# A gather kernel in which 96 rows are copied from HBM to HBM one by one, with their indices in registers

One core of one Trainium2 chip. The metric is the device time of one execution in microseconds (us), lower is better.

## The reference

```python
def setup_inputs():
    batch, seq, dim = 32, 512, 1024
    return {"x": randn(batch, seq, dim) as float32,
            "indices": randint(0, seq, (batch, 128)) as int32}

def reference(x, indices):
    for b in range(batch):
        result[b] = x[b, indices[b]]        # (32, 128, 1024) float32
```

Each of the 32 batches picks 128 rows of 4 KB out of 512. The draw is fixed; a batch has 109 to 120 distinct rows.

## The kernel before

Batches 0 to 4 are gathered whole from HBM (the chip's main memory) into SBUF (on-chip memory) and stored. From batch 5 on only distinct rows are gathered: VectorE finds repeats and gives each distinct row a slot, an indirect DMA on GpSimd fetches the slots (a slot without a row has an index out of bounds and is skipped: the trace has 3024 rows of 4 KB for the 27 x 128 slots, and 4-byte packets for the other 432), TensorE spreads the slots to the 128 output places with a 0/1 matrix, ScalarE copies the result from PSUM, where TensorE leaves it, to SBUF, and SyncE (SP) stores. Distinct rows are about 114 of 128, so this saves about a tenth of the reads. (Of batch 5 only the rows from 256 up are gathered; ScalarE's queue loads the lower 256 whole beforehand.) The table `rank` says which slot the n-th distinct row takes, so that the 16 DMA engines get the same number of rows (189 each, by the count in the prediction below).

```python
    rank = const.tile([N, 8, 16], I32, name="rank")
    for e in range(8):
        fold = 0
        for bit, col in enumerate((6, 5, 3)):
            fold ^= col * (e >> bit & 1)
        steps = [[(-16 if fold >> bit & 1 else 16) << bit, 2] for bit in (2, 1, 0)]
        nc.gpsimd.iota(rank[:, e], pattern=[[1, 2]] + steps, base=2 * e + 16 * fold, channel_multiplier=0)
    # ... cut
    def store(b):
        if b not in PAIRED:
            nc.sync.dma_start(out=of[b * N:(b + 1) * N], in_=blocks[b])
        elif b % 2:
            nc.sync.dma_start(out=of[(b - 1) * N:(b + 1) * N].rearrange("(t p) d -> p t d", t=2),
                              in_=blocks[b - 1, "pair"][:])

    for b in range(HEAD):                     # HEAD = 5
        gather(blocks[b], first[...] if b == 0 else idxT[:, b:b + 1], b)
        store(b)
    # ... cut: ranks, slots, the 0/1 matrices
    def fetch(b):
        if HEAD <= b < B:
            gather(held[(b - HEAD) % RING][:], at[:, b:b + 1], b, bounds_check=S - 1, oob_is_err=False)
    # ... cut
    for b in range(HEAD, B):
        spread_rows(b)                        # matmuls, PSUM to SBUF, store(b)
        fetch(b + RING)                       # RING = 8
```

Of the kernel before, what the change touches and what calls it, by code (L numbers as in the profile page):

```python
# [6 lines left out]
F32 = mybir.dt.float32  # L7
F16 = mybir.dt.float16
I32 = mybir.dt.int32
ALU = mybir.AluOpType  # L10
# [18 lines left out]
def kernel(ctx, tc, x, indices, out):  # L29
# [14 lines left out]
    nc = tc.nc  # L44
    B, S, D = x.shape
    N = indices.shape[1]
    HEAD, RING, GROUP, AHEAD, FAR = 5, 8, 3, 4, 1024
    HALF = HEAD
    PAIRED = range(12, 20)
    GROUPS = (B - HEAD) // GROUP  # L50
    assert 2 * N <= S <= FAR and (B - HEAD) % GROUP == 0
    const = ctx.enter_context(tc.tile_pool(name="const", bufs=1))
    ring = ctx.enter_context(tc.tile_pool(name="ring", bufs=1))
    rows = ctx.enter_context(tc.tile_pool(name="rows", bufs=1))
    pick = ctx.enter_context(tc.tile_pool(name="pick", bufs=1))
    junkp = ctx.enter_context(tc.tile_pool(name="junk", bufs=4))
    PS = bass.MemoryType.PSUM
    pbc = ctx.enter_context(tc.tile_pool(name="pbc", bufs=2, space=PS))
    psm = ctx.enter_context(tc.tile_pool(name="psm", bufs=1, space=PS))
    pout = ctx.enter_context(tc.tile_pool(name="pout", bufs=4, space=PS))  # L60
    pe, dve, act = InOrder(tc), InOrder(tc), InOrder(tc)
    mm, v = nc.tensor.matmul, nc.vector


    first = const.tile([N, 1], indices.dtype, name="first")
    nc.sync.dma_start(out=first[:], in_=indices.rearrange("b n -> n b")[:, 0:1])
    vals = const.tile([B, N], indices.dtype, name="vals")
    nc.sync.dma_start(out=vals[:], in_=indices)


    diff = const.tile([N, N], I32, name="diff")
    nc.gpsimd.iota(diff[:], pattern=[[1, N]], base=0, channel_multiplier=-1)
    rank = const.tile([N, 8, 16], I32, name="rank")
    for e in range(8):
        fold = 0
        for bit, col in enumerate((6, 5, 3)):
            fold ^= col * (e >> bit & 1)
        steps = [[(-16 if fold >> bit & 1 else 16) << bit, 2] for bit in (2, 1, 0)]
        nc.gpsimd.iota(rank[:, e], pattern=[[1, 2]] + steps, base=2 * e + 16 * fold, channel_multiplier=0)
    less = const.tile([N, 1], F32, name="less")  # L80
    zero = const.tile([N, 1], F32, name="zero")
    dve(v.memset, zero[:], 0.0)
# [4 lines left out]
    above = const.tile([N, N], F16, name="above")  # L87
    dve(v.tensor_scalar, out=above[:], in0=diff[:], scalar1=0, scalar2=None, op0=ALU.is_gt)
    dve(v.tensor_copy, out=less[:], in_=diff[:, 0:1])
    every = const.tile([N, N], F16, name="every")  # L90
    dve(v.memset, every[:], 1.0)
    turn = const.tile([N, N], F16, name="turn")
    dve(v.tensor_copy, out=turn[:], in_=rank[:].rearrange("p e q -> p (e q)"))
    vf = const.tile([N, N], F16, name="vf")
    dve(v.memset, vf[:], 0.0)
    dve(v.tensor_copy, out=vf[:B],
        in_=vals[:].bitcast(I32).rearrange("p (n two) -> p n two", two=2)[:, :, 0])
# [4 lines left out]
    for k in range(2):  # L102
        load = act(nc.scalar.dma_start, out=early[k][:], in_=xf[HALF * S + k * N:HALF * S + (k + 1) * N])
        if k == 0:
# [7 lines left out]
    idxT = const.tile([N, B], I32, name="idxT")  # L112
# [3 lines left out]
    near = const.tile([N, B], F16, name="near")  # L116
    dve(v.tensor_scalar, out=near[:], in0=tr[:], scalar1=float(-FAR), scalar2=None, op0=ALU.add)

    of = out.flatten_outer_dims()

    def gather(dst, at, b, **kw):
        nc.gpsimd.indirect_dma_start(  # L122
            out=dst, out_offset=None,
            in_=xf[:], in_offset=bass.IndirectOffsetOnAxis(ap=at, axis=0),
            element_offset=b * S * D, **kw)


    blocks = {}
    for b in range(B):
        if b not in PAIRED:  # L130
            blocks[b] = rows.tile([N, D], F32, name=f"block{b}")[:]
# [4 lines left out]

    def store(b):
        if b not in PAIRED:
            nc.sync.dma_start(out=of[b * N:(b + 1) * N], in_=blocks[b])
        elif b % 2:  # L140
            nc.sync.dma_start(out=of[(b - 1) * N:(b + 1) * N].rearrange("(t p) d -> p t d", t=2),
                              in_=blocks[b - 1, "pair"][:])

    for b in range(HEAD):
        gather(blocks[b], first[:].bitcast(I32)[:, 0:1] if b == 0 else idxT[:, b:b + 1], b)
        store(b)

    def table(name, dtype):
        return const.tile([N, B], dtype, name=name)

    cnt, lead, slot = table("cnt", F32), table("lead", F16), table("slot", F16)
    nth, at = table("nth", I32), table("at", I32)
    past = const.tile([N, B + 1], F16, name="past")
    dve(v.memset, past[:, HEAD:HEAD + 1], 0.0)
    bcs, packs, spread = {}, {}, {}

    def of_group(g):
        return range(HEAD + g * GROUP, HEAD + (g + 1) * GROUP)

    def cols(t, g):  # L160
        return t[:, HEAD + g * GROUP:HEAD + (g + 1) * GROUP]

    def wide(t):
        return t.rearrange("p (g o) -> p g o", o=1).to_broadcast([N, GROUP, N])

    def step0(g):

# [3 lines left out]
        for k, b in enumerate(of_group(g)):  # L171
            junk = junkp.tile([N, N], F16, name="junk")
            dve(v.scalar_tensor_tensor, out=junk[:], in0=bc[:, k], scalar=idxF[:, b:b + 1], in1=below[:],
                op0=ALU.is_equal, op1=ALU.mult, accum_out=cnt[:, b:b + 1])
        if HALF in of_group(g):
            c = slice(HALF, HALF + 1)
            dve(v.scalar_tensor_tensor, out=cnt[:, c], in0=idxF[:, c], scalar=2.0 * N, in1=cnt[:, c],
# [4 lines left out]

    def step1(g):

        rk = psm.tile([N, GROUP], F32, name="rk")
        pe(mm, rk[:], lhsT=above[:], rhs=cols(lead, g), start=True, stop=False)
        pe(mm, rk[:], lhsT=every[:], rhs=cols(past, g), start=False, stop=True)
        dve(v.tensor_copy, out=cols(nth, g), in_=rk[:])
        dve(v.tensor_scalar, out=cols(nth, g), in0=cols(nth, g), scalar1=N - 1, scalar2=None, op0=ALU.bitwise_and)
        dve(v.scalar_tensor_tensor, out=cols(slot, g), in0=cols(cnt, g), scalar=256.0, in1=cols(nth, g),  # L190
            op0=ALU.mult, op1=ALU.add)
        packs[g] = pack = junkp.tile([N, GROUP, N], F16, name="pack")
        dve(v.tensor_tensor, out=pack[:], in0=turn[:].rearrange("p (o n) -> p o n", o=1).to_broadcast([N, GROUP, N]),
            in1=wide(cols(slot, g)), op=ALU.is_equal)

    def step2(g):

        pos = psm.tile([N, GROUP], F32, name="pos")
        for k, b in enumerate(of_group(g)):
            pe(mm, pos[:, k:k + 1], lhsT=packs[g][:, k], rhs=near[:, b:b + 1], start=True, stop=True)  # L200
        dve(v.tensor_scalar, out=cols(at, g), in0=pos[:], scalar1=float(FAR), scalar2=None, op0=ALU.add)
        s = pick.tile([N, GROUP, N], F32, name=f"s{g}")
        dve(v.tensor_tensor, out=s[:], in0=bcs[g][:, :GROUP], in1=wide(cols(at, g)), op=ALU.is_equal)
        for k, b in enumerate(of_group(g)):
            spread[b] = s[:, k]

    def fetch(b):
        if HEAD <= b < B:
            gather(held[(b - HEAD) % RING][:], at[:, b:b + 1], b, bounds_check=S - 1, oob_is_err=False)

    held = []
# [5 lines left out]
    def half_spread():  # L217

        same = pick.tile([N, 2, N], F32, name="same")
        for k in range(2):  # L220
            dve(v.tensor_scalar, out=same[:, k], in0=bcs[0][:, HALF - HEAD], scalar1=less[:], scalar2=float(k * N),
                op0=ALU.add, op1=ALU.is_equal)
        spread[HALF, "early"] = [same[:, k] for k in range(2)]

    def half_rows(h, last):
        w = slice(h * 512, (h + 1) * 512)
        if not last:
            spread[HALF, h] = pout.tile([N, 512], F32, name="ps")
        ps = spread[HALF, h]
        if last:  # L230
            pe(mm, ps[:], lhsT=spread[HALF], rhs=held[(HALF - HEAD) % RING][:, w], start=False, stop=True)
        else:
            for k in range(2):
                pe(mm, ps[:], lhsT=spread[HALF, "early"][k], rhs=early[k][:, w], start=k == 0, stop=False)
        if last:
            nc.scalar.copy(out=blocks[HALF][:, w], in_=ps[:])  # L236

    def spread_rows(b):
        for h in range(2):
            if b == HALF:  # L240
                half_rows(h, True)
                continue
            w = slice(h * 512, (h + 1) * 512)
            ps = pout.tile([N, 512], F32, name="ps")
            pe(mm, ps[:], lhsT=spread[b], rhs=held[(b - HEAD) % RING][:, w], start=True, stop=True)
            nc.scalar.copy(out=blocks[b][:, w], in_=ps[:])  # L246
        store(b)

    step0(0)
    step0(1)  # L250
    for g in range(AHEAD):
# [8 lines left out]
            half_spread()  # L260
        elif g < 3:
            half_rows(g - 1, False)
    for b in range(HEAD, B):
        spread_rows(b)
        fetch(b + RING)
        g, step = divmod(b - HEAD, GROUP)
        if g + AHEAD < GROUPS:
            (step0, step1, step2)[step](g + AHEAD)
# [30 lines left out]
```

## Time and profile before

| | before |
|---|---|
| time, median | 88.11 us (87.52 to 88.28) |
| span of the profiled run | 85.4 us |
| bytes moved, mean rate | 32.91 MB, 385 GB/s |
| 4 KB packets for one DMA engine | 501, each 159 ns |
| DMAs issued by SP | 2 loads and 28 stores |

The prediction below shows the lines for the DMA engines, stage by stage. One more view: the list of instructions that touch the output. Columns: issuing line and queue, operation, count, then the shortest, median and longest time that the issuing sequencer spends on one (ns), then start of the first and the last (us):

```profile
L139 SPq DMA_DIRECT2D out_dram<-block x24: 332/332/360, 7.2 to 78.4; - x24
L141 SPq DMA_DIRECT2D out_dram<-pair x4: 372/374/387, 40.9 to 52.3; - x4
```

### The profile page before, as it was taken

The page shows a single profiled execution, that of the slowest core. Times are in us where ns is not written, and L with a number is a line of the kernel's source. Part 1 is how long each engine was busy: PE and PEld are TensorE (multiplying, and loading weights), DVE is VectorE, ACT ScalarE, POOL GpSimd, SP SyncE. Part 2 cuts the span into 40 slices and gives each one's busy share as a digit, 9 for nine tenths or more (in the row PEclk, how much of TensorE's full clock was granted, in tenths as well). Part 3 has the DMA queues.
Part 4 walks back from the last instruction along what each step waited for, and adds up shares of the span by engine and source line. Part 5 has one row for each costly group of instructions (what it writes and reads, how often), then busy time and mean ns, then how long its engine had stood idle before and what let it go on. Part 6 is the DMA issues. An engine that isn't in the chain of part 4 may idle for free.

```text
span 85.4 us, 829 instructions
## 1 busy us (share of the span) xinstructions
PE 61.1 (72%) x189; PEld 25.5 (30%) x189; DVE 31.7 (37%) x160; ACT 40.6 (48%) x63; POOL 33.9 (40%) x45
## 2 busy tenths in 40 slices
PE   0310379460999999999999999997879988884000
PEld 0300142220434444354444444442212333320000
DVE  3698892864318547375485473000000000000000
ACT  0999920000145566656655666675553454445000
POOL 7687777837024554444555544466000000000000
PEclk9999999999569999999999999999999999999655
DMA  0999999999999999999999999999999999999990
GB/s 1 319 401 263 259 405 413 417 413 426 416 416 424 411 420 420 413 428 418 411 424 416 411 418 418 416 424 418 413 424 418 413 428 413 418 424 418 414 372 23
DMA packets 9636, 32.91 MB, mean 385 GB/s; under 512 B 1584, under 2 KB 1616, under 8 KB 9632
## 3 DMA queue, kind: packets, MB, share of 16 engines
q1 hardware_dynamic: 4736, 16.81, 48.3%
q0 software_dynamic: 4608, 15.01, 45.0%
q10 hardware_dynamic: 288, 1.05, 3.4%
q8 instruction: 1, 0.02, 0.1%
q14 instruction: 3, 0.02, 0.1%
HBM read 17.86 MB, written 16.78 MB: 406 GB/s over the span
## 4 chain that ended last, share of the span: by engine, by line
PE 39%; DMA 21%; DVE 11%; issue 8%; POOL 7%; another core or an unknown queue 2%; ACT 1%; POOLq 1%; SPq 0%; DVEq 0%
PE ps L24 36%; DMA u<-in_x_dram,at 20%; POOL u L122 7%; DVE junk L24 3%; DMA vals<-in_indices_dram 2%; DVE past L24 2%; PE bc L24 2%; DVE pack L24 1%; DVE s L24 1%; DVE nth L24 1%; PE pos L24 1%; DVE lead L24 1%; ACT block L246 1%; DVE same L24 1%
## 5 line engine op out<-in xcount | busy, mean ns | idle before, releaser
L24 PE MATMUL ps<-u,s 128*128 128x512 f32 x108 | 52.8, 624 | 3.4 <-DMA u<-in_x_dram,at 3.4
L122 POOL DMA_INDIRECT u<-in_x_dram,at x27 | 26.9, 998 | 23.8 <-PE ps L24 7.2
L246 ACT COPY block<-ps 128x512 f32<-128x512 f32 x36 | 21.1, 586 | 16.5 <-PE ps L24 15.4
L24 PEld LDWEIGHTS ps<-u,s 128*128 128x128 f32 x108 | 18.9, 193 | 24.7 <-issue 13.4
L246 ACT COPY pair<-ps 128x512 f32<-128x512 f32 x16 | 9.4, 586 | 5.8 <-PE ps L24 4.2
L24 DVE SCALAR_TENSOR_TENSOR junk<-bc,idxF,below 128x128 f16<-128x128 f32 x27 | 8.0, 347 | 7.9 <-PE bc L24 7.9
L24 ACT COPY u<-zero 128x1024 f32<-128x1024 f32 x8 | 7.7, 1040 | 0.0
L236 ACT COPY block<-ps 128x512 f32<-128x512 f32 x2 | 1.2, 586 | 13.2 <-PE ps L24 13.2
L24 PE MATMUL pos<-near,pack 128*128 128x1 f16 x27 | 2.0, 167 | 7.4 <-DVE nth L24 2.9
L24 PE MATMUL ps<-early,same 128*128 128x512 f32 x8 | 5.7, 855 | 0.0
L24 DVE TENSOR_TENSOR pack<-turn,slot 128x384 f16<-128x384 f16 x9 | 5.0, 558 | 0.3
L24 DVE TENSOR_TENSOR s<-bc,at 128x384 f32<-128x384 f32 x9 | 5.0, 557 | 0.3
L24 PEld LDWEIGHTS <-pack 128*128 128x128 f16 x27 | 1.7, 99 | 11.2 <-DVE pack L24 4.3
L24 DVE TENSOR_TENSOR past<-past,lead 128x1 f16<-128x1 f16 x27 | 4.4, 163 | 0.9
L122 POOL DMA_INDIRECT block<-in_x_dram,idxT x4 | 4.1, 1036 | 1.2 <-issue 0.9
L24 PE MATMUL bc<-vf,ident 128*128 128x128 f16 x27 | 3.5, 257 | 1.3 <-DVE same L24 1.3
L24 PEld LDWEIGHTS <-ident 128*128 128x128 f16 x27 | 2.5, 114 | 4.9 <-issue 4.9
L24 DVE TENSOR_SCALAR at<-pos 128x3 int32<-128x3 f32 x9 | 1.4, 160 | 4.2 <-PE pos L24 3.5
L24 DVE CAST nth<-rk 128x3 int32<-128x3 f32 x9 | 1.4, 159 | 4.0 <-PE rk L24 1.9
L21 PE MATMUL pos<-ident,vf 128*128 128x32 f16 x1 | 0.2, 208 | 3.2 <-DVE vf L24 3.2
L24 PE MATMUL rk<-lead,above 128*128 128x3 f16 x9 | 1.6, 172 | 1.1 <-DVE lead L24 1.1
L24 ACT ACT_TABLE_LOAD x1 | 1.3, 1283 | 2.2 <-DVE ident L24 2.2
(31 smaller groups left out, 18.4 us busy)
## 6 DMA issues: line engine op xcount, KB each, us to landing
out_dram<-block SPq DMA_DIRECT2D x24, 512.0 KB
out_dram<-pair SPq DMA_DIRECT2D x4, 1024.0 KB
early<-in_x_dram ACTq DMA_DIRECT2D x2, 512.0 KB
u<-in_x_dram,at POOLq DMA_INDIRECT x27
block<-in_x_dram,idxT POOLq DMA_INDIRECT x4
vals<-in_indices_dram SPq DMA_DIRECT2D x1, 32.0 KB
first<-in_indices_dram SPq DMA_DIRECT2D x1, 1.0 KB
block<-in_x_dram,first POOLq DMA_INDIRECT x1
```

The costliest lines, as they stand in the source:

```text
L21: self.last = do(*args, **kw)
L24: self.last = do(*args, **kw)
L122: nc.gpsimd.indirect_dma_start(out=dst, out_offset=None, in_=xf[:], in_offset=bass.IndirectOffsetOnAxis(ap=at, axis=0), element_offset=b * ...
L236: nc.scalar.copy(out=blocks[HALF][:, w], in_=ps[:])
L246: nc.scalar.copy(out=blocks[b][:, w], in_=ps[:])
```

## The change

The intent: a row that goes from HBM to HBM directly passes a DMA engine once, not twice (gather, then store); e4 below has one packet of 159 ns for such a row. So 96 rows of the last batch are copied by 96 single DMAs, whose source row is an index loaded into a register. The author of the change assumes that such a copy falls on DMA engine 0, and gives that engine fewer gathered rows. The rows are issued by SP, three after each store. The diff, cut to its core:

```diff
+    LONE = B - 1
+    BEGIN = 32
+    MAIN = N - 5
...
-    rank = const.tile([N, 8, 16], I32, name="rank")
-    (six lines cut)
+    rank = const.tile([N, 2, 64], I32, name="rank")
+    nc.gpsimd.iota(rank[:], pattern=[[60, 2], [2, 8], [1, 2], [15, 4]], base=-1, channel_multiplier=0)
+    nc.gpsimd.iota(rank[:, :, :4], pattern=[[4, 2], [1, 4]], base=120, channel_multiplier=0)
...
+    def go_alone():
+        for n in range(BEGIN, N, LOAD):                        # LOAD = 8
+            loads, at_rows = nc.values_load_multi_w_load_instructions(
+                flat[LONE:LONE + 1, n:n + LOAD], engines=[mybir.EngineType.SP], min_val=0, max_val=S - 1,
+                skip_runtime_bounds_check_because="the indices are rows of a batch")
+            for k, row in enumerate(at_rows):
+                nc.sync.dma_start(out=out[LONE, n + k:n + k + 1], in_=x[LONE][bass.ds(row, 1)])
+                yield
...
     for b in range(HEAD):
         gather(blocks[b], ...)
         store(b)
+        rows_alone(3)
+    gather(blocks[LONE][:BEGIN], idxT[:BEGIN, LONE:LONE + 1], LONE)
+    sp(nc.sync.dma_start, out=of[LONE * N:LONE * N + BEGIN], in_=blocks[LONE][:BEGIN])
+    rows_alone(12)
...
         store(b)                                               # in spread_rows
+        rows_alone(3)
...
-    for b in range(HEAD, B):
+    for b in range(HEAD, LONE):
```

Also changed, and cut here: groups of three batches are counted from the other end, and some small VectorE instructions compute a rank modulo 123 instead of 128.

## The prediction

The forecast's sum: 78.3 us for each engine before; 73.5 + 1.2 + 14.9 = 89.6 us for engine 0 after, +11.3, taken as +12; 88.18 + 12 = 100 us. That the 96 rows (14.9 us) fall on the engine with 165 gathered rows was an assumption, taken over from the change: the kernel before has no one-row copy. "Engine 0" and "engine 8" are names for the engines of slots 0-3, 32-35 and of 64-67, 96-99; the packet records carry no engine number. Rival 2, with the trace's 159 ns for a gathered and for a stored row, would be an estimated 318 ns.

> **What bounds the kernel now.** I read the page's 40 slices first, then the queue table and the chain, then a table of stages, the DMA queue's own waits and last the packet records of the trace.

> ```profile
> PE   0310379460999999999999999997879988884000
> ...
> DMA  0999999999999999999999999999999999999990
> GB/s 1 319 401 263 259 405 413 417 413 426 416 416 424 411 420 420 413 428 418 411 424 416 411 418 418 416 424 418 413 424 418 413 428 413 418 424 418 414 372 23
> DMA packets 9636, 32.91 MB, mean 385 GB/s; under 512 B 1584, under 2 KB 1616, under 8 KB 9632
> ...
> q1 hardware_dynamic: 4736, 16.81, 48.3%
> q0 software_dynamic: 4608, 15.01, 45.0%
> q10 hardware_dynamic: 288, 1.05, 3.4%
> ```

> The DMA engines are over 90% busy from the second slice to the next to last, at a nearly flat 411 to 428 GB/s once the stores run. PE looks busy too, but a busy PE is not proof of a bound, and the stages tell more. The columns are start:end, length, busy time of PE, its weight loads, DVE, ACT and POOL, then clock, DMA share, GB/s:

> ```profile
> 6.00:11.00 5.00, 0.77 (x8) 0.45 (x8) 4.29 (x20) 5.00 (x6) 3.64 (x4) 1.00 0.95 278
> 11.00:16.00 5.00, 4.08 (x12) 1.66 (x12) 2.99 (x17) 0.16 (x1) 4.00 (x4) 1.00 1.03 415
> 40.00:60.00 20.00, 19.50 (x62) 8.55 (x61) 7.38 (x34) 12.35 (x22) 10.97 (x11) 1.00 1.03 418
> 60.00:80.00 20.00, 14.83 (x31) 4.93 (x29) 0.00 (x0) 9.38 (x16) 0.00 (x0) 0.99 1.03 419
> ```

> From 60 to 80 us POOL and DVE are done, PE and ACT have gaps, and the rate stays 419 GB/s: the bytes set the end. The chain agrees. It names much PE in the middle, but its last long piece is the last gather, issued at 58.96 us and waiting 16.67 us in a full queue:

> ```profile
> 58.96 16.67 DMA u<-in_x_dram,at
> 75.77 1.97 PE ps L24 x4
> 77.76 0.59 ACT block L246
> ```

> So the kernel is 16 DMA engines' worth of packets plus a start of some 3 us. The packet records (start, duration, size, queue; no engine number) give the unit: 8016 packets of 4 KB, 501 for each engine; one lasts 159 ns, and following single engines through the trace, one 4 KB packet starts 155.3 ns after the other (a 4-byte one costs 6 ns). 501 x 155.3 = 77.8 us, and about 89 small ones x 6 = 0.5 us: **78.3 us** for each engine. 88.18 us leaves 9.9 us of start, slow first gathers (278 GB/s), tail and launch, which I carry over. What counts hence is the packets of the **busiest single engine**, for a store is done when its slowest engine is.

> [...] This the trace lets me test, since a gather's skipped rows (index out of bounds) show as 4-byte packets. I recomputed from the indices which rows are skipped and followed engines by the 155 ns step from 18 to 32 us. For nine of the 16 engines the sequence could be followed without a break, and in all nine all 70 packets compared agree with groups {p..p+3, p+32..p+35}. With {p..p+3, p+64..p+67} the best fit of each is 64 to 66 of 70. The grouping stands[...]. [...]

> **The change part by part.**

> *Removed.* The last batch (113 distinct rows) is no longer gathered whole and stored whole: 113 + 128 packets. It keeps 32 gathered and 32 stored. Also gone: one POOL gather (1.0 us), 4 matmuls and 2 ACT copies (0.59 us each), a few iotas. None of the engine work is on the path that sets the end, apart from the bytes.

> *Added on the DMA engines.* 96 single rows that pass an engine once instead of twice. Spread evenly, the total would be 8016 - 241 + 64 + 96 = 7935, 496 an engine, 5 packets or 0.8 us less: the gain aimed at, about 1%.

> *Added on SP.* 96 copies with a register address and 12 loads of eight registers. A store costs SP 332 ns (the tile view), so an estimate of 96 x 0.35 = 34 us plus some 10 us. SP has room: it waits 30.1 + 13.4 + 8.0 us for ACT in the waits below, and per batch three rows and a store come to about 1.7 us of 2.4.

> ```profile
> SPq L139 <- ACT block L246: 30.1, 18, 2.1
> SPq L141 <- ACT pair L246: 13.4, 4, 3.4
> SPq L139 <- ACT block L236: 8.0, 1, 8.0
> ```

> *Moved: who gathers what.* This is the step that decides. The old order of ranks gave each engine exactly 189 gathered rows of batches 5 to 31[...] (recomputed: 189 on all 16; 16 x 189 = 3024 = 3664 whole q0 packets less the 640 of five full gathers). The new one frees slots 0-3 and 64-67, as if one engine served both. By the grouping that the trace confirmed they belong to two: recomputed for batches 5 to 30, engine 0 still gets **165**, engine 8 gets **96**, the others 186 to 192. (Had the trace shown 0-3 with 64-67, engine 0 would get 72 and the others 189 or 190: the layout is plainly meant for that.) Every engine besides has 40 of the first five gathers, 2 of the new short one, 16 of the early loads, 250 of the stores: 308.

> - Engines 9 to 15: 192 + 308 = 500 packets, 77.7 us. As before.
> - Engine 8: 96 + 308 = 404.
> - Engine 0: 165 + 308 = 473, 73.5 us; about 202 small packets (96 semaphores among them) x 6 = 1.2 us; 96 rows x 155 ns = 14.9 us. Sum **89.6 us**, against 78.3: +11.3 us.

> If an HBM-to-HBM row takes longer than one with SBUF, each further 10 ns adds 1.0 us. I take 160 to 170 ns, so about +12 us: the path must read and write HBM, and the first gathers show reads that are slower than 159 ns on average (205 to 244 ns between 2 and 10 us).

> Does the excess lie on the path? The rows stand in the same queue as the stores, three after each store, so engine 0's stores fall back behind those of the others, while gathers, in another queue, go on. No block is used twice, so nothing stops SP from queueing. Engine 0 then has work without a gap from the first stores on and ends last; its whole sum is the time. 88.18 + 12 = **100 us**.

> **Rivals.**
> 1. *The rows land on engine 8, or the layout fits the hardware after all.* For it: a tuned kernel's author would have seen a loss of 12 us, and 96 + 96 = 192 would be in balance. Against it: [...]the diff's own words (engine 0), the nine followed engines. It would give 500 packets at the most, hence 87 to 89 us; up to 91 if rows are slow.
> 2. *An HBM-to-HBM row costs about as much as its read and its write.* [...]
> 3. *A row is cut into 16 pieces of 256 B over all engines.* For it: 1024 elements divide by 16. The trace has 1 KB packets of 44 ns, so about 20 ns and a 6 ns semaphore each, 96 x 26 = 2.5 us on every engine, against no saving on the busiest: about 90.5 us.
> 4. *SP becomes the bound.* If a row costs SP 0.7 us and a register load more than I think, three rows and a store pass 2.4 us and stores come late from the eighth batch on: +5 to +14 us, also slower. For it: no instruction in the profile shows such a cost. Against it: SP's 50 us of waiting.

> **Range and chances.** Engine 0 overloaded, 0.70: most of it between 98 and 105[...]. SP bound without that, 0.05: slower as well. Rivals 1 and 3 and unknown placements, 0.25: mostly 86.5 to 90. Faster by over 2% needs a time under 86.4, which even the even spread (-0.8 us) does not reach: 0.04. The point, 100, is the middle of the main case; 88 to 110 leaves out the very slow row and half of the balanced cases.

> **What would show it.** Right: moved bytes down by about 1% (q0 less by some 81 rows, q1 with 4096 whole packets still), but mean GB/s down to about 330; in the 40 slices a stretch of DMA busy share well under 9 at the end, about 23 GB/s (one engine) for several us; PE and ACT done long before the end; the chain ending in a store or a row, and SP waiting at the end for out_dram. The last packets come from one engine, 155 ns or more apart. The lasting time of the new packets gives the row's cost. Wrong: GB/s flat near 418 to the end (rival 1); some 1500 packets of 256 B (rival 3); DMA share low all through with SP never waiting (rival 4); row packets of about 300 ns (rival 2).

## More of the kernel before

SP hands over 128 rows in 332 ns. It has 28 such orders between 7.2 and 78.4 us, and is idle for most of that time. The engine table of a page does not count this: issuing a DMA is not "busy".

## The result, and the profile after

**122.42 us** median (122.29 to 122.61) against 88.11 us. A ratio here and below is the mean time of one kernel's fast runs over that of the other's fast runs of the same rounds, so not quite the ratio of the medians quoted: 1.393, 95% interval 1.386 to 1.399. Slower, as expected, but by 34 us, not 12.

The page after, the lines that answer to those of before:

```profile
DMA  2979999999877989999999925362373535534475
GB/s 32 347 254 302 408 377 394 395 401 397 276 228 212 304 281 391 380 403 391 395 378 382 407 76 219 136 272 83 132 288 125 208 137 196 205 132 180 179 315 208
DMA packets 12520, 32.62 MB, mean 271 GB/s; under 512 B 4641, under 2 KB 4673, under 8 KB 12512
...
q1 hardware_dynamic: 7712, 16.82, 36.0%
q0 software_dynamic: 4512, 14.68, 34.5%
```

Two things differ from what I had described. First, about 3000 more packets are under 512 B (4641 against 1584). The packet records show why: 1536 packets of 256 B (median 18 ns), so each row was cut into 16 pieces, and 1536 more 4-byte semaphore packets (9 ns). Up to 7 of the pieces are under way at one time, so they do not all stand on one engine. Second, the low DMA share does not belong to one engine at the end: from the 24th slice on the rate jumps between 76 and 315 GB/s for 50 us. The stages:

```profile
9.00:76.00 67.00, 58.85 (x183) 25.11 (x183) 31.25 (x160) 32.82 (x55) 28.40 (x28) 0.97 0.92 337
76.00:116.00 40.00, 0.00 (x0) 0.00 (x0) 0.00 (x0) 0.16 (x1) 0.00 (x0) 0.55 0.44 173
```

From 76 to 116 us the compute engines do next to nothing (one ACT instruction, 0.16 us), and the DMA engines are at 0.44. All data is computed and lies in SBUF. Something else keeps the stores back. The chain of waits does not see it; its last pieces end at 76.2 us of 120.5:

```profile
56.54 19.02 PE ps L24 x44
75.58 0.59 ACT block L282
```

The chain follows busy instructions, and SP's issuing is none. What helps is SP's own queue in order of time (start, length from the first of a group to the end of its last, what, count):

```profile
92.32 0.53 SPq L24 DMA_DIRECT2D out_dram<-block  x1
93.05 1.97 SPq L155 DMA_DIRECT2D out_dram<-in_x_dram  x3
95.11 0.53 SPq L24 DMA_DIRECT2D out_dram<-block  x1
95.84 2.59 SPq L155 DMA_DIRECT2D out_dram<-in_x_dram  x3
98.53 0.53 SPq L24 DMA_DIRECT2D out_dram<-block  x1
...
114.15 1.82 SPq L24 DMA_DIRECT2D out_dram<-block  x3
```

Store, three rows, store, three rows, without a pause: 2.79 us for a batch, 3.42 where eight registers are loaded in between. And the waits of that queue, which had 30.1 + 13.4 + 8.0 us for ACT before:

```profile
SPq L24 <- DMA block<-in_x_dram,first: 6.5, 1, 6.5
SPq L24 <- DMA out_dram<-block: 3.9, 5, 1.1
...
SPq L24 <- ACT block L282: 0.5, 2, 0.3
```

SP no longer waits for ACT (0.5 us); ACT's results wait for SP. The list of instructions on the output:

```profile
L155 SPq DMA_DIRECT2D out_dram<-in_x_dram x96: 512/518/1219, 9.9 to 113.5; - x96
L24 SPq DMA_DIRECT2D out_dram<-block x24: 338/526/729, 8.2 to 115.2; - x24
```

Handing over one row of 4 KB takes 518 ns, more than a store of 512 KB took before (332 ns), and a store that follows such rows takes 526 ns. I added up SP's instruction records from the start of its first store at 8.2 us to the start of its last at 115.2 us, 107.1 us in all (the sum is rounded):

| SP, changed kernel | us |
|---|---|
| handing over 96 rows (mean 572 ns) | 55.0 |
| 12 loads of eight registers (mean 955 ns) | 11.5 |
| 192 register instructions for the addresses | 7.4 |
| handing over 27 stores (means 484 and, for pairs, 528 ns) | 13.0 |
| short gaps between these, under 150 ns each | 14.8 |
| waits (the nine longer gaps) | 5.5 |

In the kernel before, the same stretch lasts 71.2 us, and 60 us of it is waiting. Without waits a row costs SP 0.90 us (issue, registers, its share of a load, gaps). So much the trace says. Experiments must show which part matters, and whether the engines, the new ranks or the small packets have a share.

### The profile page after: what moved, and what is told of

The parts are those of the page before. It is cut to its first block, busy times and chain, and to the rows that moved or that the text cites. A ratio compares the mean times of both kernels' runs of the same rounds, so it can differ in the third digit from the quotient of the medians.

```text
span 120.5 us, 1165 instructions
## 1 busy us (share of the span) xinstructions
PE 60.0 (50%) x192; PEld 25.8 (21%) x192; DVE 36.5 (30%) x194; ACT 39.4 (33%) x61; POOL 33.4 (28%) x39
## 2 busy tenths in 40 slices
DMA packets 12520, 32.62 MB, mean 271 GB/s; under 512 B 4641, under 2 KB 4673, under 8 KB 12512
## 3 DMA queue, kind: packets, MB, share of 16 engines
q10 hardware_dynamic: 288, 1.05, 2.6%
## 4 chain that ended last, share of the span: by engine, by line
PE 41%; DVE 16%; issue 2%; DMA 1%; POOL 1%; ACT 0%
PE ps L24 38%; DVE pack L24 4%; DVE turns L24 4%; DVE nth L24 3%; PE pos L24 2%; DMA first<-in_indices_dram 1%; DVE slot L24 1%; DVE junk L24 1%; POOL block L126 1%; PE bc L24 1%; DVE past L24 1%; PE rk L24 1%; ACT block L282 0%; DVE same L24 0%; DVE lead L24 0%
## 5 line engine op out<-in xcount | busy, mean ns | idle before, releaser
L24 PE MATMUL ps<-u,s 128*128 128x512 f32 x104 | 49.6, 619 | 0.0
L282 ACT COPY block<-ps 128x512 f32<-128x512 f32 x34 | 19.9, 586 | 12.1 <-PE ps L24 11.1
L24 PEld LDWEIGHTS ps<-u,s 128*128 128x128 f32 x104 | 19.0, 195 | 17.6 <-issue 16.4
L24 DVE SCALAR_TENSOR_TENSOR junk<-bc,idxF,below 128x128 f16<-128x128 f32 x26 | 7.7, 347 | 7.4 <-PE bc L24 7.4
L24 ACT COPY u<-zero 128x1024 f32<-128x1024 f32 x8 | 7.7, 1040 | 0.0
L24 PE MATMUL ps<-early,same 128*128 128x512 f32 x8 | 7.1, 1046 | 0.0
L24 PE MATMUL pos<-near,pack 128*128 128x1 f16 x26 | 2.1, 170 | 8.8 <-DVE pack L24 8.2
L272 ACT COPY block<-ps 128x512 f32<-128x512 f32 x2 | 1.2, 586 | 15.7 <-PE ps L24 15.7
L126 POOL DMA_INDIRECT block<-in_x_dram,idxT x5 | 4.7, 932 | 2.6 <-DVE idxF L24 1.4
L24 DVE TENSOR_TENSOR pack<-turn,slot 128x384 f16<-128x384 f16 (+1 forms) x9 | 4.9, 544 | 0.3
L24 DVE TENSOR_TENSOR s<-bc,at 128x384 f32<-128x384 f32 (+1 forms) x9 | 4.9, 542 | 0.3
L24 DVE TENSOR_TENSOR past<-past,lead 128x1 f16<-128x1 f16 x26 | 4.2, 162 | 0.9
L24 PEld LDWEIGHTS <-pack 128*128 128x128 f16 x26 | 1.3, 100 | 13.7 <-DVE pack L24 13.7
L24 PE MATMUL bc<-vf,ident 128*128 128x128 f16 x26 | 3.5, 265 | 1.1 <-DVE same L24 1.1
L24 PEld LDWEIGHTS <-ident 128*128 128x128 f16 x26 | 2.4, 116 | 4.7 <-issue 4.7
L24 PEld LDWEIGHTS <-above 128*128 128x128 f16 x18 | 1.9, 111 | 6.1 <-issue 6.1
L24 PEld LDWEIGHTS ps<-early,same 128*128 128x128 f32 x8 | 2.4, 324 | 2.1 <-issue 2.1
L24 DVE TENSOR_SCALAR turns<-rk 128x3 f32<-128x3 f32 (+1 forms) x9 | 1.4, 158 | 4.4 <-PE rk L24 4.1
L24 PE MATMUL rk<-lead,above 128*128 128x3 f16 (+1 forms) x18 | 1.8, 169 | 1.0 <-DVE lead L24 1.0
```

The lines of the kernel that those rows point to most:

```text
L24: self.last = do(*args, **kw)
L126: nc.gpsimd.indirect_dma_start(out=dst, out_offset=None, in_=xf[:], in_offset=bass.IndirectOffsetOnAxis(ap=at, axis=0), element_offset=b * ...
L272: nc.scalar.copy(out=blocks[HALF][:, w], in_=ps[:])
L282: nc.scalar.copy(out=blocks[b][:, w], in_=ps[:])
```

## The experiments

**Theory A**: SP is the bound; it is held by the rows, and the stores stand behind them. **B**: the new ranks and the longer VectorE work cost the time. **C**: my prediction, engine 0 has too many packets. **D**: the small packets and semaphores fill the DMA engines. Runs marked "wrong" give a wrong output.

### e1: no single rows

```diff
-    BEGIN = 32
+    BEGIN = N
```

> The changed kernel without any single-row copy: the last batch is gathered whole (128 rows) and stored whole, everything else of the change stays. Theory A (SyncE is the bound: row copies of about 0.69 us each stand before the stores in its queue): 89 to 91 us, for SP is idle again; the busiest DMA engine has 192+40+8+16+256 = 512 packets against 501, about 1.7 us more than before. Rival B (the new order of ranks and the longer DVE chain cost the time): stays above 110 us. Rival C (my prediction, engine 0 overloaded by the rows): also about 90.

90.62 us (before 88.60; ratio 1.017, 1.010 to 1.025). B falls as the main cause: ranks, groups and VectorE work together with 11 more packets an engine cost 2.0 us of 34 (1.5 by the ratio). The other 32 us belong to the rows.

### e2: the stores of batches 5 to 30 on ScalarE's queue

```diff
-            sp(nc.sync.dma_start, out=of[b * N:(b + 1) * N], in_=blocks[b])
+            (nc.sync if b < HEAD else nc.scalar).dma_start(out=of[b * N:(b + 1) * N], in_=blocks[b])
```

(and the same for pairs)

> The changed kernel with the stores of batches 5 to 30 issued by ScalarE instead of SyncE; the 96 row copies stay on SyncE. Theory A: the stores no longer stand behind rows, SP has 96 x 0.69 + 12 loads x 0.9 + 6 stores x 0.7 = 81 us of its own work from about 10 us on, so 91 to 96 us. Rival B (ranks, DVE): stays near 122. Rival C/D (the rows' 1536 small packets and their semaphores, or engine 0, hold the DMA engines): stays above 110, for the same packets run.

114.56 us (ratio 1.282). My 91 to 96 was a miss. The list of instructions on the output, and SP's queue in order of time:

```profile
L155 SPq DMA_DIRECT2D out_dram<-in_x_dram x96: 512/518/1310, 9.7 to 110.2; - x96
L143 ACTq DMA_DIRECT2D out_dram<-block x18: 338/339/361, 28.5 to 105.1; - x18
...
28.01 82.72 SPq L155 DMA_DIRECT2D out_dram<-in_x_dram  x81
```

81 rows with no store between them took SP 82.7 us, 1.02 us a row, of which 7.4 us in all are waits. I had put in 0.69 us, read off three rows in a row without a load, and 0.9 us for each load of eight, which is 0.80 us a row. So the rows alone keep SP until 110 us: the run does not show SP free, it shows SP as the bound even without the stores. That answers little on D by itself. It also shows a new coupling: ACT waited 15.9 + 5.7 us for row copies, with which the rows have nothing to do as data. The reason is in e4.

### e3: fixed rows instead of registers (wrong)

```diff
-            for k, row in enumerate(at_rows):
-                nc.sync.dma_start(out=out[LONE, n + k:n + k + 1], in_=x[LONE][bass.ds(row, 1)])
+            for k in range(LOAD):
+                row = (n + k) * 37 % S
+                sp(nc.sync.dma_start, out=out[LONE, n + k:n + k + 1], in_=x[LONE, row:row + 1])
```

> Wrong on purpose: the 96 rows are copied from fixed rows of the batch, so no register loads and no register addresses; number, size and place of the copies stay. Theory A with the register as the cost: a row costs SP about what a store cost before (0.33 to 0.4 us), SP needs about 50 us in all, and the time is 89 to 92 us (the small packets cost each DMA engine an estimated 96 x 24 ns = 2.3 us). Theory A with the copy's issue itself as the cost: rows stay at 0.6 to 0.7 us and the time stays above 105. Rival D (small packets): stays near 122.

110.55 us (ratio 1.234). Two of the four runs are slow; the fast ones have a mean of 109.6. So registers and loads are worth some 13 us of the 34 (122.4 less 109.6). The larger part stays with plain copies. (The 24 ns in the expectation is an estimate: 18 ns for a packet of 256 B in the change's trace and 6 for its semaphore, which by the records takes 9.)

### e4: fixed rows that aren't cut (wrong)

As e3, with `[..., :1021]` on both sides: 1021 is a prime number.

> Wrong on purpose: as the fixed rows, but 1021 of 1024 elements (a prime, so that the copy can't be cut into 16 pieces): 96 packets of 4084 B instead of 1536 of 256 B. This is the case that I predicted: if all fall on engine 0, and it still has its 165 gathered rows, 98 to 104 us, with DMA busy share well under 9 in a tail and one engine's rate. If they fall on the engine that has 96 gathered rows, or on an engine made free by the new ranks: 88 to 91 us. If SP is the bound here too: above 105.

### e7 and e10: one copy of 89 rows (wrong)

89 is prime, and I expected that all rows go through one engine; the tail at 26 GB/s below agrees. SP issues one DMA.

```diff
+        sp(nc.sync.dma_start, out=out[LONE, BEGIN:BEGIN + 89], in_=x[LONE, 0:2 * 89:2])
```

e10 adds the slots that the trace of before suggests for engine 0:

```diff
-    nc.gpsimd.iota(rank[:], pattern=[[60, 2], [2, 8], [1, 2], [15, 4]], base=-1, channel_multiplier=0)
-    nc.gpsimd.iota(rank[:, :, :4], pattern=[[4, 2], [1, 4]], base=120, channel_multiplier=0)
+    for h in range(2):
+        for half in range(2):
+            nc.gpsimd.iota(rank[:, h, half * 32:half * 32 + 32], pattern=[[1, 8], [15, 4]],
+                           base=8 * h - 1 + 60 * half, channel_multiplier=0)
+    nc.gpsimd.iota(rank[:, 0, 0:4], pattern=[[1, 4]], base=120, channel_multiplier=0)
+    nc.gpsimd.iota(rank[:, 0, 32:36], pattern=[[1, 4]], base=124, channel_multiplier=0)
```

> Wrong on purpose: 89 fixed rows (a prime number, so that all go through one DMA engine) in ONE copy from HBM to HBM instead of 96 copies, so SP is free; 7 rows are never written. This is the DMA side of my prediction by itself. If the copy falls on engine 0 with its 165 gathered rows: 165+40+2+16+250+89 = 562 packets, 87.9 us of engine time against 78.3 before, 97 to 100 us. If it falls on the engine with 96 gathered rows, or slot groups are as the change assumes: 493 at most, 500 elsewhere, 88 to 90 us.

> As e7, but the slots that get few rows are 0-3 and 32-35 (the groups that the trace of the kernel before shows) instead of 0-3 and 64-67: 72 gathered rows on that engine, 189 or 190 on the others. If that engine is the one the copy falls on: 500 packets at most, 87.5 to 89.5 us, some 9 to 10 us under e7. If not: no better than e7.

e7: 97.39 us (ratio 1.104, 1.095 to 1.112). e10: 90.20 us (ratio 1.018, 1.010 to 1.027). The rate in 40 slices, first e7:

```profile
GB/s 10 307 354 263 313 368 332 363 370 375 387 384 408 415 399 398 337 370 375 349 389 404 397 415 415 415 408 416 418 415 422 416 423 397 409 415 165 26 26 7
```

then e10:

```profile
GB/s 0 240 385 242 264 342 407 344 368 412 290 396 416 420 420 418 414 414 420 405 410 412 405 414 412 425 418 418 416 418 423 418 418 418 420 416 423 405 183 6
```

e7 ends with two slices (2.4 us each) at 26 GB/s, which is one engine: 4096 B / 159 ns = 25.8 GB/s. With slots 0-3 and 32-35 spared, that tail is gone, and 7.2 us with it. So this copy, which isn't cut, does fall on the engine of slots 0-3 and 32-35, and the slots of the change (0-3 and 64-67) spare half of two engines. That was my prediction's mechanism, and it is there, but only where the copy isn't cut, which it is in the change. The size: 562 - 500 = 62 packets x 155 ns is 9.6 us, and 7.2 were measured. e10 landed 0.7 us above its range; e8, which has 500 packets as well, came to nearly the same (89.9), so the changed preparation may cost some 1.4 to 1.7 us beyond its packets. But e1 leaves only 0.3 us for it (2.0 us less 1.7 for 11 packets).

### e8: the rows replaced by register loads (wrong)

```diff
+                    loads, got = nc.values_load_multi_w_load_instructions(
+                        flat[LONE:LONE + 1, n + k:n + k + 1], engines=[mybir.EngineType.SP], ...)
+                    sp.last = nc.sync.keepalive_nop(ins=list(loads[0].ins.outs))
```

> Wrong on purpose: each row copy is replaced by one register load on SP whose value nobody uses: SP is held about as long (I expect 0.6 to 1.3 us for one) but issues no DMA, so no completion semaphore is taken. Theory A1 (SP's own time is all): SP is held 96 x load + 31 x 0.34; at 0.65 us a load that is 73 us from 8 us on, 90 to 93 us; at 1.0 us 107 us on SP and 115 to 120 us in all. Theory A2 (each row takes one of eight completion semaphores, and SP waits for the DMA that had it before; that is most of the 18 us of the fixed rows): the time is what the sum of SP's held time says, without any wait of SP for out_dram.

89.94 us (ratio 1.018). The instruction list and the queue's waits:

```profile
L153 SPq TENSOR_LOAD <-flat x96: 273/519/1952, 8.6 to 80.8; - x96
...
SPq L24 <- ACT block L283: 1.5, 3, 0.8
SPq L24 <- ACT pair L283: 1.2, 3, 0.5
```

From its first to its last store (74.4 us) SP is held almost all of the time: the loads have a mean of 596 ns, the rows of e4 had 598. No wait for `out_dram` is left before the end. e1 is no fair measure, for it has 12 more packets an engine; e10 has the same 500 and an SP that mostly waits, and takes 90.20 us. So holding SP for some 74 us costs nothing: it fits into the idle time that SP had. It only just fits, for near the end the DMA engines are not kept fully busy (the last digits of the line):

```profile
DMA  0898999999999999999999999999999999986593
```

### e11: e4 without the overload of engine 0 (wrong)

e8 and e4 differ by more than waits, since e4 may have its 96 packets on the overloaded engine 0, as e7 had its 89 (not read off e4's records). e11 is e4 with the ranks of e10.

> Wrong on purpose: e4 (96 copies of fixed rows, one packet each) with the slot groups 0-3 and 32-35 of e10. e7 against e10 showed that engine 0 was overloaded; e4 had that too. If the overload of engine 0 makes SP wait for late stores and so most of e4's 106.6 us: 91 to 94 us here. If it is the eight completion semaphores taken in turn, whatever engine is loaded: 103 to 107 us.

106.06 us (ratio 1.203): the same as e4. The overload of engine 0 is not what makes SP wait. SP's waits and the instruction list:

```profile
SPq L24 <- DMA out_dram<-block: 12.6, 11, 2.1
...
SPq L24 <- DMA out_dram<-pair: 1.4, 1, 1.4
...
L24 SPq DMA_DIRECT2D out_dram<-in_x_dram x96: 555/572/1757, 8.3 to 97.7; - x96
```

Against e8: SP's stretch is 91.3 us instead of 74.4, of which waits are 14.0 us (against none for DMAs) and longer issues most of the rest. The times differ by 16.1 us, with practically the same packets (at most 500 and 498 for one engine). So with SP's slack already used up by holding, the waits for the eight semaphores go straight into the time. Their number was not varied, so the share of the waits is read from the trace. Nor does a run hold SP for the change's 102 us without row DMAs; that step rests on the sum of SP's records above.

### e5: registers, and rows that aren't cut (wrong)

This is the change as its words have it: one packet on one engine. `[..., :1021]` in the changed kernel.

> Wrong on purpose: the changed kernel with 1021 of 1024 elements of each row, so each copy is one packet on one engine, as the words of the change have it; registers and loads stay. SP is held 102 us between its first and last store in the changed kernel; here the stores are issued faster after such copies (0.36 instead of 0.48 us, seen in e4), some 4 us less, and a row's issue is as long: 116 to 121 us, a little under the changed kernel. If the cutting into 16 pieces was what cost SP its time: 100 to 108 us, as e4.

126.95 us (ratio 1.446), slower than the change itself; my 116 to 121 was a miss. Stores were issued faster, as expected (mean 360 instead of 484 ns), but the rows were slower (622 instead of 572 ns) and so were the loads (1297 instead of 955 ns; I don't know why). The cut into 16 pieces is not what cost SP its time. D falls too: without the 1536 small packets the kernel gets no faster, and in the change itself the DMA engines are at 0.44 from 76 to 116 us.

### e6: half the rows

```diff
-    BEGIN = 32
+    BEGIN = 80
```

> The changed kernel with 48 single rows instead of 96 (the first 80 rows of the last batch are gathered). SP issue alone: 48 x 0.69 + 6 loads x 0.9 + 31 stores x 0.6 = 57 us, well under the 78 us at which the kernel before issues its last store. Theory A as a threshold (SP only costs when it is behind at the end): 91 to 95 us, since the rows run out by batch 12 and SP catches up. If the cost is the same for each row (linear between 90.6 without rows and 122.4 with 96): 106 us.

95.89 us (ratio 1.083), correct output. Just above my range and far from the linear 106.

```profile
GB/s 8 314 351 259 308 357 311 340 417 414 397 409 400 356 274 210 237 292 334 329 341 394 373 383 400 383 374 340 410 416 422 419 422 417 421 422 419 419 386 40
```

After its rows have run out at 65 us SP catches up, and the rate is 416 to 422 GB/s to the end. But the dip from the 14th to the 20th slice, where 12 rows in a row stand before the store of batch 5, isn't made up by the end.

### e9: the ceiling of the idea (wrong)

The kernel before, with the last batch as one plain copy of 128 fixed rows from HBM to HBM.

```diff
+    with tc.issue_after(stored.ins):
+        nc.sync.dma_start(out=out[B - 1], in_=x[B - 1, 0:2 * N:2])
...
-    for b in range(HEAD, B):
+    for b in range(HEAD, B - 1):
```

(`fetch` stops one batch earlier too)

> Wrong on purpose: the kernel BEFORE with the whole last batch copied from HBM to HBM by one plain copy of 128 fixed rows (8 packets on each engine) in place of its gather and store. The ceiling of the idea: 501 - 15 + 8 = 494 packets an engine, 1.1 us less, so a ratio of 0.985 to 0.99 if a row from HBM to HBM takes 159 ns on all engines at once; about 1.00 or above if it takes longer than 300 ns.

87.09 us against 87.99 (ratio 0.988, 0.982 to 0.994). SP hands the whole batch over in one piece:

```profile
L148 SPq DMA_DIRECT2D out_dram<-in_x_dram x1: 613/613/613, 17.5 to 17.5; - x1
```

The arithmetic of the change agrees: seven packets fewer for each engine (15 less and 8 more, if the 128 rows are spread evenly), 1.1 us, where the interval allows 0.5 to 1.6. 613 ns for 128 rows, against about 570 for one: here the cost is for the order, not for the rows. But fixed rows are no solution.

## Why the prediction was wrong

- **What bounds the kernel before: right.** The DMA engines; e9 moves the time by about what it takes away in packets.
- **Direction: right, but by luck: the mechanism did not decide.** I said that rows fall on engine 0, which still has 165 gathered rows. e7 and e10 show that mechanism (7.2 us). In the change it can't act as I reckoned, for each row is cut into 16 pieces of 256 B, of which up to 7 are under way at one time. I took "one packet on engine 0" for given, which nothing in the trace before showed, and left the cut as rival 3, within 0.25 for all balanced cases.
- **"Added on SP": the step that failed.** I put a row at 0.35 us because a store cost 0.332, and the loads at 10 us: 44 us in all, well inside 50 us of idle time. Measured: 572 ns for the issue alone, 0.90 us with registers, loads and gaps, 86 us in all, and stores at 484 ns instead of 335. That is twice the term, and it is beyond SP's slack. I named this as rival 4, "+5 to +14", and gave it 0.05.
- **"Nothing stops SP from queueing": wrong.** Each plain DMA waits for the one eight before it (120 of 120 in the change's trace). In the change SP has only 5.5 us of waits of any kind, because it is late anyway; where SP is just full, the waits for landings are 14.0 us (e11).
- **The cost of a row on an engine: nearly right.** Median 159 ns, mean 178 (e4), where I took 160 to 170; rival 2, a row at the cost of its read and its write (2 x 159 = 318 ns), is refuted. Two small readings do not come out of the records: a 4-byte packet lasts 9 ns, not 6 (0.6 us at most on engine 0), and 4 KB packets of the first 10 us average 164 ns from 4 to 6 us, not 205 to 244 throughout.
- **The size of the loss.** e1, e11, e3 and the change make a ladder: 90.6 us without rows; 106 with 96 single orders of fixed rows; 109.6 (fast runs) if each is cut into 16; 122.4 with registers and their loads. Rungs of different experiments need not add up.

What stays open: why a plain order from HBM to HBM holds SP longer (555 ns and up) than one from SBUF (332 ns), why loads took longer in e5, and what the preparation costs (0.3 to 1.7 us).

## What to carry to other kernels

Count orders as well as bytes: a queue that has 28 DMAs to issue and waits 50 us is not a queue that can take 96 more, until one has the cost of one such order (here 0.9 us with its registers) and has asked what each order must wait for (here the landing of the eighth before it). The profile counts issuing nowhere as busy; when every engine is idle and the chain of waits ends long before the span, read the issuing queue in order of time. And a gain of 5 packets an engine (0.8 us) leaves no room for a second mistake, so measure its ceiling first with a wrong-on-purpose kernel like e9.
